# Post-norm work of the first tokens dealt out over the last FFN product, hidden pieces split earlier, and more matmuls between norm sums and their spread

## The chip, the core and the metric

The kernel runs on one core of a Trainium2 chip. A core has a matrix engine (TensorE, PE in the profile, its weight loads PEld), a vector engine (VectorE, DVE), a scalar engine (ScalarE, ACT), GpSimd (POOL) and SyncE (SP), each with an instruction queue of its own; they wait for one another through semaphores, and sixteen DMA engines move data. The metric is the device time of one execution in microseconds.

## What is computed

Two layers of a transformer over 512 tokens of width 1024, all in float32. Layer 0 attends with low-rank queries and keys (8 heads), layer 1 attends over chunks to keys and values projected once from the end of layer 0 (16 heads). Each layer ends in the same feed-forward network. Every sub-layer is normed before and after:

```python
for layer in range(DEPTH):
    h = rms_norm(x, attn_pre_g[layer])
    y = mla_mixer(h, ...) if layer < N_A_LAYERS else chunked_mixer(h, k_band, v_band, ...)
    x = x + rms_norm(y, attn_post_g[layer])
    h = rms_norm(x, ffn_pre_g[layer])
    f = swiglu(h, ffn_w_gate[layer], ffn_w_up[layer], ffn_w_down[layer])
    x = x + rms_norm(f, ffn_post_g[layer])
    if layer == N_A_LAYERS - 1:
        k_band, v_band = shared_kv(x, kv_src_g, w_kv_shared)
```

with `swiglu(h, g, u, d) = (silu(h @ g) * (h @ u)) @ d`, a hidden width of 2816, and `rms_norm(x, g) = x * rsqrt(mean(x*x) + 1e-6) * g`.

## The kernel before

**Products.** A float32 product is made of three matmuls (`mm3`, L351 to L354): both operands are split into a rounded half and the rest, high by high, low by high and high by low are added in PSUM. For that each weight is cast by ScalarE to `whi` (L144), and VectorE takes the rest, `wlo = w - whi` (L145). Where a gain is folded in, the same is done by L148 and L149. Activations are split likewise, as `xh`/`xl`, `th`/`tl` or `ph`/`pl`.

**The order.** The code is written as one program; a scheduler then sets the order of the instructions on each engine from the program's order and its own estimates, and each engine runs its queue strictly in that order. So an instruction that waits holds all that stands behind it on its engine. Generators (`some(gen, n)` runs n steps, `run(gen)` the rest; `Filler.step` one step) lay the matmuls of one product around other work.

**Norm sums.** A norm over the features needs a sum over partitions. VectorE adds squares into `acc` (L422), TensorE sums `acc` over partitions with transposes or ones (`tot`, L431), `rstd` (L436) makes `r` with GpSimd's power (L448), and `spread` (L461) transposes `r` back over all partitions (`bc`, L465). Between `tot` and `bc` stand a few matmuls of the running product: `add_half(h, banks, rest, n1, n2)` (L571) runs n1 steps ahead of the sum and n2 steps between sum and spread; in `ffn` (L1064) it is `some(rest, 4)`, and at the start of layer 1's values (L1435) `spread_sb(rtk)` comes as soon as `rtk` is there.

**The down product.** `down` (L1149) multiplies the hidden values by the down weights with seven products instead of eight of half the size, in the order A11, A22, A12, E1, E2, E3, E6 (j = 0 to 6). Each has six weight tiles in five groups, the last group with two, and is 66 matmuls of 128x512 into two PSUM banks (al, de, ga, be, al, al, be). Ahead of each tile `hid.ahead(n)` (L1104) splits the hidden pieces up to step n into `ph` and `pl`; before, n is two steps ahead. Behind each group the post-norm object is called with `during(j, i)`, and behind each product with `product(j, banks)`.

**The post-norm.** `After` (L1204) puts the seven products together: `copy` (L1218) takes a bank into `y`, `plus` (L1223) adds another and squares (`sq`, L1228). The tokens stand in four tiles of 128, the outputs in two halves o. Behind E3 the first two token tiles are whole: `plus(1, 0)`, `rstd(0)` and `plus(1, 1)` follow at once. `power` (L1257) makes `r` from the two sums (ssv, L1260 and L1261; power on GpSimd, L1263) and calls `scale`, in layer 0 on ScalarE (L1270). Then `turn(h)` (L1279) transposes the scaled y (`yt`, L1288) and adds it to x (L1291); `turn(0)` is called in E6 behind the fourth tile (i == 3), `turn(1)` inside the value product of layer 1 (L1425). The residual `x` comes back from memory by `fetch(a["mid"])` (L608), called in E1 at i == 3.

`AfterLast` (L1295), for layer 1, has no next product. It transposes the residual x into rows (`xt`, L1316, copied by L1318) during E2 at i = 1 to 4, two tiles a group, multiplies y by the gain (`yg`, L1322), and `scale` (L1335) multiplies by r, adds xt and stores a tile of 256 KB (L1336).

## Time and profile before

| | |
|---|---|
| three runs | 1150.61, 1150.11 and 1149.77 us, median 1150.11 |
| the profiled execution | 1152.78 us, its span 1151.0 us |
| mean granted TensorE clock | 0.992 |
| seven down products, layer 0 and 1 | the last of them is E6, 513.88 to 536.55 and 1119.77 to 1142.33 |
| data moved | 149.80 MB, 130 GB/s in the mean |

Times in the trace count from the start of the span. A row of the timeline has its start, its length, engine, line, operation, what it writes and reads, the shape and the number of like instructions merged in it; in brackets stands the idle time of the engine before it and what ended that. A row of the waits has who waited for whom, the sum, the number and the longest. A row of windows has the length, then for PE, PEld, DVE, ACT and POOL the busy time with the number of instructions, then the granted TensorE clock, the DMA share and GB/s. Matmuls are pipelined: one 128x512 is shown as 0.39 us long, and the next starts 0.23 us later.

### The profile page before, as it was taken

To read this page: it belongs to the slowest core of one execution; us is meant where nothing else is said; L and a number is where in the kernel's file an instruction comes from. 1 tells how busy PE (TensorE), PEld (TensorE's weight loads), DVE (VectorE), ACT (ScalarE), POOL (GpSimd) and SP (SyncE) were. 2 spreads that over 40 slices of the span, in tenths; PEclk is the share of its full clock that TensorE was granted. 3 is DMA by queue.
4 is the path that set the end of the run, shared out by engine and by line. 5 is a ranking of instruction groups with operands and counts; after the bars stand their busy time and mean duration, and the time that the engine had idled before them with its cause. 6 is when DMAs were issued, how large, how long until landed. Compare 5 with 4: busy or idle time off the path is not lost.

```text
span 1151.0 us, 18964 instructions
## 1 busy us (share of the span) xinstructions
PE 1120.8 (97%) x6973; PEld 993.7 (86%) x6973; DVE 936.2 (81%) x1674; ACT 684.1 (59%) x1335; POOL 63.2 (5%) x90
## 2 busy tenths in 40 slices
PE   9999999999999999999999999999999999999995
PEld 6888889899999998777788887789899999998774
DVE  7787638999898889878768877748999898889866
ACT  6476646755555566668436766655655555556662
POOL 1200000000000003300000000000000000004200
PEclk9999999999999999998999999999999999999998
DMA  7433134322323359922446656444323323369701
GB/s 230 119 108 100 38 120 173 128 74 93 129 92 123 97 172 252 235 67 95 137 135 163 171 151 166 128 165 138 101 93 102 102 92 129 102 219 230 164 1 74
DMA packets 62270, 149.80 MB, mean 130 GB/s; under 512 B 8352, under 2 KB 9888, under 8 KB 62176
## 3 DMA queue, kind: packets, MB, share of 16 engines
q1 hardware_dynamic: 55696, 137.00, 37.9%
q0 software_dynamic: 6336, 11.54, 6.1%
q8 instruction: 55, 0.90, 0.3%
q14 instruction: 39, 0.32, 0.1%
q10 hardware_dynamic: 144, 0.04, 0.0%
HBM read 119.52 MB, written 8.59 MB: 111 GB/s over the span
## 4 chain that ended last, share of the span: by engine, by line
PE 80%; DVE 8%; issue 5%; ACT 4%; DMA 2%; POOL 1%; SPq 0%; DVEq 0%; POOLq 0%; ACTq 0%
PE al L1366 18%; PE b L352 10%; PE b L353 10%; PE b L354 9%; PE be L1366 9%; PE al L1169 5%; PE ga L1366 5%; PE be L1169 3%; PE de L1169 2%; PE pt L504 2%; DVE wlo L145 2%; PE ga L1169 1%; ACT whi L144 1%; ACT p L492 1%; DVE pl L145 1%
## 5 line engine op out<-in xcount | busy, mean ns | idle before, releaser
L144 ACT CAST whi<-raw 128x1024 fp32r<-128x1024 f32 (+3 forms) x224 | 225.3, 1006 | 234.0 <-PE al L1366 82.9
L145 DVE TENSOR_TENSOR wlo<-raw,whi 128x1024 fp32r<-128x1024 f32 (+3 forms) x224 | 260.7, 1164 | 74.6 <-ACT whi L144 71.8
L1366 PE MATMUL al<-th,whi 128*128 128x256 f32 x432 | 124.1, 287 | 0.0
L1366 PE MATMUL al<-tl,whi 128*128 128x256 f32 x432 | 122.2, 283 | 0.0
L1366 PE MATMUL al<-th,wlo 128*128 128x256 f32 x432 | 122.1, 283 | 0.0
L352 PE MATMUL b<-xh,whi 128*128 128x512 f32 (+1 forms) x304 | 116.3, 385 | 0.4 <-ACT xh L148 0.3
L353 PE MATMUL b<-xl,whi 128*128 128x512 f32 (+1 forms) x304 | 113.0, 372 | 0.0
L354 PE MATMUL b<-xh,wlo 128*128 128x512 f32 (+1 forms) x304 | 112.9, 371 | 0.0
L174 DVE TENSOR_TENSOR raw<-raw,raw 128x1024 f32<-128x1024 f32 x72 | 86.5, 1217 | 0.2
L1366 PEld LDWEIGHTS al<-th,whi 128*128 128x128 f32 x432 | 82.7, 191 | 1.8
L1366 PEld LDWEIGHTS al<-th,wlo 128*128 128x128 f32 x432 | 82.8, 192 | 0.0
L1366 PEld LDWEIGHTS al<-tl,whi 128*128 128x128 f32 x432 | 82.7, 191 | 0.0
L492 ACT ACTIVATE p<-p,mn 128x128 f32<-128x128 f32 (+1 forms) x96 | 54.0, 562 | 31.6 <-DVE mn L490 31.2
L144 ACT CAST whi<-wd 128x512 fp32r<-128x512 f32 x86 | 50.0, 619 | 37.9 <-PE al L1169 13.7
L145 DVE TENSOR_TENSOR ptl<-pt,pth 128x128 fp32r<-128x128 f32 (+1 forms) x96 | 46.2, 485 | 28.7 <-ACT pth L144 23.1
L145 DVE TENSOR_TENSOR wlo<-wd,whi 128x512 fp32r<-128x512 f32 x86 | 56.2, 684 | 14.9 <-ACT whi L144 14.7
L354 PEld LDWEIGHTS b<-xh,wlo 128*128 128x128 f32 x304 | 57.5, 189 | 8.9
L352 PEld LDWEIGHTS b<-xh,whi 128*128 128x128 f32 x304 | 57.7, 190 | 8.6 <-ACT xh L148 1.7
L353 PEld LDWEIGHTS b<-xl,whi 128*128 128x128 f32 x304 | 57.7, 190 | 7.5 <-DVE xl L149 0.7
L144 ACT CAST pth<-pt 128x128 fp32r<-128x128 f32 (+1 forms) x96 | 40.3, 424 | 28.4 <-PE pt L504 27.7
L1169 PE MATMUL al<-whi,ph 128*128 128x512 f32 x132 | 52.0, 394 | 2.9 <-ACT y L1218 1.6
L1169 PE MATMUL al<-whi,pl 128*128 128x512 f32 x132 | 51.4, 392 | 0.2
(304 smaller groups left out, 3277.9 us busy)
## 6 DMA issues: line engine op xcount, KB each, us to landing
raw<-in_w_pair SPq DMA_DIRECT2D x72, 512.0 KB, 3.5
wd<-in_w_down SPq DMA_DIRECT2D x54, 256.0 KB, 6.0
raw<-in_w_o SPq DMA_DIRECT2D x16, 512.0 KB, 3.6
raw<-in_w_gu SPq DMA_DIRECT2D x16, 512.0 KB, 3.8
raw<-in_w_down SPq DMA_DIRECT2D x16, 512.0 KB, 4.4
raw<-in_w_qkb SPq DMA_DIRECT2D x16, 512.0 KB, 3.5
wd<-in_w_down POOLq DMA_DIRECT2D x22, 256.0 KB, 5.2
wd<-raw POOLq DMA_DIRECT2D x22, 256.0 KB, 5.3
```

Source lines behind the costliest of these rows:

```text
L144: return (nc.scalar.copy(dst_hi, src), V.tensor_tensor(dst_lo, src, dst_hi.bitcast(F32), op=OP.subtract))
L145: V.tensor_tensor(dst_lo, src, dst_hi.bitcast(F32), op=OP.subtract))
L174: V.tensor_tensor(t, x, y, op=OP.add)
L352: nc.tensor.matmul(o, l[0], r[0], start=start, stop=False)
L353: nc.tensor.matmul(o, l[0], r[1], start=False, stop=False)
L354: nc.tensor.matmul(o, l[1], r[0], start=False, stop=stop)
L492: nc.scalar.activation(p[:, :n], p[:, :n], AF.Exp, bias=mn[:, :1], scale=-1.0, accum_out=self.sums[:, qt:qt + 1])
L504: nc.tensor.transpose(t[:, kt * P:(kt + 1) * P], p[:, kt * P:(kt + 1) * P], ident)
L1169: nc.tensor.matmul(to[e], l[c], r[d], start=j < 4 and k == 0 and n == 0, stop=k == NF // 2 - 1 and n == 2, skip_group_check=True)
L1366: nc.tensor.matmul(o, l[c], r[d], start=first_ and n == 0, stop=k == K2 - 1 and n == 2, skip_group_check=True)
```

## The change

Five things are edited.

1. `add_half` in the output projection takes 8 and 5 steps in place of 5 and 7: three steps more ahead of the sum, two fewer between the sum and its spread.
2. In `ffn`, 7 steps in place of 4 stand between the sum of the pre-norm and its spread. The spread of `rtk` in layer 1 moves behind seven steps of the filler.
3. `hid.ahead` splits pieces three steps ahead in E2 and E3 and four steps ahead in E6, in place of two.
4. `After` puts `plus(1, 1)` and the scaling of the first two token tiles on a list, `later`; each group of E6 takes one of them off the list. `fetch` is called at i == 1 of E1.
5. `AfterLast` makes each pair of `xt` a group earlier, deals the work out as `After` does, multiplies the o = 1 half of the first two token tiles by its gain in `scale`, and scales and stores the very last tile in two halves.

```diff
-                    post.add_half(0, before, rest, 5, 7)
+                    post.add_half(0, before, rest, 8, 5)
...
-        some(rest, 4)
+        some(rest, 7)
         rb = spread_sb(r)
...
-                    hid.ahead(at + 2 - len(got))
+                    hid.ahead(at + (2, 2, 2, 2, 3, 3, 4)[j] - len(got))
...
             elif j == Down.E3:
                 self.plus(1, 0, banks)
                 self.rstd(0)
-                self.plus(1, 1, banks)
+                self.later = [lambda: self.plus(1, 1, banks)] + self.later
...
             for e in range(n):
-                self.scale(i + e, r[:, e:e + 1])
+                do = lambda e=e: self.scale(i + e, r[:, e:e + 1])
+                self.later.append(do) if i < 2 else do()
...
         def during(self, j, i):
-            if j == Down.E1 and i == 3:
+            if j == Down.E1 and i == 1:
                 self.x = fetch(a["mid"])
                 self.split = Split(self.x, None)
+            if j == Down.E6 and self.later:
+                self.later.pop(0)()
             if j == Down.E6 and i == 3:
                 self.turn(0)
...
-            super().during(j, -1 if j == Down.E6 else i)
+            super().during(j, min(i, 2))
...
-            if j == Down.E2 and i:
-                for n in {1: (0, 1), 2: (2, 3), 3: (4, 5), 4: (6, 7)}[i]:
+            if j == Down.E2 and i < 4:
+                for n in (2 * i, 2 * i + 1):
...
         def whole(self, o, i):
+            if o and i < 2:
+                return
+            self.gained(o, i)
+            if i >= 2 and not o:
+                self.power(i, 1)
+
+        def gained(self, o, i):
             t = U(name="yg")
             V.tensor_tensor(t, self.y[o][i], self.g[o], op=OP.mult)
             self.y[o][i] = t
 
-            if i >= 2 and not o:
-                self.power(i, 1)
...
         def scale(self, i, r):
-            for o in (1, 0) if i >= 2 else (0, 1):
+            if i < 2:
+                self.gained(1, i)
+            for o in (1, 0):
                 t = self.y[o][i]
-                V.scalar_tensor_tensor(t, t, r, self.xt[i][o], op0=OP.mult, op1=OP.add)
-                nc.sync.dma_start(out[:, i, o * S:o * S + S], t)
+                for c in HALF if i == 3 and not o else (ALL,):
+                    V.scalar_tensor_tensor(t[:, c], t[:, c], r, self.xt[i][o][:, c], op0=OP.mult, op1=OP.add)
+                    nc.sync.dma_start(out[:, i, o * S:o * S + S][:, c], t[:, c])
...
-    rb = spread_sb(rtk)
...
     fill = Filler(fill_b())
+    for _ in range(7):
+        fill.step()
+    rb = spread_sb(rtk)
```

How this moves instructions, at three places.

ScalarE in E6 of layer 0, before. `y_...<-y_...,r` are the scalings of the first two token tiles, `sq` the squares of y, `ph` the pieces of the coming tiles:

```order
L1228 ACTIVATE sq_5957,ss_0_5086<-y_5398 128x512
L1228 ACTIVATE sq_5968,ss_0_5086<-y_5701 128x512
L1228 ACTIVATE sq_5971,ss_0_5086<-y_5703 128x512
L1270 ACTIVATE y_5234<-y_5234,r_5961 128x512
L1270 ACTIVATE y_5396<-y_5396,r_5961 128x512
L1270 ACTIVATE y_5236<-y_5236,r_5961 128x512
L1270 ACTIVATE y_5398<-y_5398,r_5961 128x512
L144 CAST ph_5973<-hd_3081 128x256
L144 CAST ph_5973<-hd_3330 128x256
L144 CAST whi_6015<-wd_5262 128x512
```

The same place of the changed kernel:

```order
L144 CAST ph_5981<-hd_4816 128x256
L1228 ACTIVATE sq_6012,ss_0_5086<-y_5701 128x512
L144 CAST whi_6021<-wd_5262 128x512
L144 CAST whi_6021<-wd_5264 128x512
L1271 ACTIVATE y_5234<-y_5234,r_5967 128x512
L1228 ACTIVATE sq_6015,ss_0_5086<-y_5703 128x512
L144 CAST ph_6017<-hd_5077 128x256
L1271 ACTIVATE y_5396<-y_5396,r_5967 128x512
L144 CAST whi_6043<-wd_5290 128x512
L144 CAST whi_6043<-wd_5292 128x512
L1271 ACTIVATE y_5236<-y_5236,r_5967 128x512
L1271 ACTIVATE y_5398<-y_5398,r_5967 128x512
```

The four scalings now stand apart and behind six more casts of pieces. On TensorE the first transposes of the scaled y stand behind 48 matmuls of E6, before behind 12.

TensorE in the first products of layer 0's FFN; `tot` stands ahead of these rows, `bc` is the spread of the pre-norm's r. It is one piece of the difference:

```order
 L353 MATMUL b_2632<-xl_2232,whi_2375 128x512
 L354 MATMUL b_2632<-xh_2231,wlo_2376 128x512
-L465 MATMUL bc_2674<-ident,r_2658 128x128 x4
 L352 MATMUL b_2633<-xh_2231,whi_2375 128x512
 L353 MATMUL b_2633<-xl_2232,whi_2375 128x512
```

and nine matmuls further on:

```order
 L353 MATMUL b_2633<-xl_2238,whi_2636 128x512
 L354 MATMUL b_2633<-xh_2237,wlo_2637 128x512
+L465 MATMUL bc_2689<-ident,r_2658 128x128 x4
 L352 MATMUL b_2632<-xh_2243,whi_2636 128x512
 L353 MATMUL b_2632<-xl_2244,whi_2636 128x512
```

The spread moved behind nine more matmuls of the same product.

VectorE at the end of the program, before; `be` are the two banks of the last product, `yg` the output tiles:

```order
L1223 TENSOR_TENSOR y_12624<-y_12624,be_11828 128x512
L1322 TENSOR_TENSOR yg_12911<-y_12624,g_11858 128x512
L1261 SCALAR_TENSOR_TENSOR ssv_11823<-ss_1_11821,ssv_11823 128x1
L1335 SCALAR_TENSOR_TENSOR yg_12779<-yg_12779,r_12915,xt_12580 128x512
L1335 SCALAR_TENSOR_TENSOR yg_12911<-yg_12911,r_12915,xt_12573 128x512
L1223 TENSOR_TENSOR y_12626<-y_12626,be_11829 128x512
L1322 TENSOR_TENSOR yg_12924<-y_12626,g_11858 128x512
```

and in the changed kernel, with the dealt-out work of the sixth weight tile ahead of it:

```order
L1332 TENSOR_TENSOR yg_12868<-y_12139,g_11860 128x512
L1345 SCALAR_TENSOR_TENSOR yg_12297<-yg_12297,r_12768,xt_12523 128x512
L1345 SCALAR_TENSOR_TENSOR yg_12868<-yg_12868,r_12768,xt_12530 128x512
L145 TENSOR_TENSOR wlo_12875<-wd_12063,whi_12874 128x512
L1223 TENSOR_TENSOR y_12628<-y_12628,be_11828 128x512
L1223 TENSOR_TENSOR y_12630<-y_12630,be_11829 128x512
L1332 TENSOR_TENSOR yg_12911<-y_12628,g_11858 128x512
L1261 SCALAR_TENSOR_TENSOR ssv_11823<-ss_1_11821,ssv_11823 128x1
L1332 TENSOR_TENSOR yg_12924<-y_12630,g_11858 128x512
L1345 SCALAR_TENSOR_TENSOR yg_12815<-yg_12815,r_12915,xt_12564 128x512
L1345 SCALAR_TENSOR_TENSOR yg_12911<-yg_12911,r_12915,xt_12557 128x512
```

Both additions of the last banks now stand ahead of the scaling, and scalings of the first tokens stand between the last two `wlo`.

## The prediction

> **What bounds the kernel now.** I read first the page's busy line and its chain, then the list of waits, then windows of equal work beside each other. The page:

> ```profile
> span 1151.0 us, 18964 instructions
> PE 1120.8 (97%) x6973; PEld 993.7 (86%) x6973; DVE 936.2 (81%) x1674; ACT 684.1 (59%) x1335; POOL 63.2 (5%) x90
> PE 80%; DVE 8%; issue 5%; ACT 4%; DMA 2%; POOL 1%; SPq 0%; DVEq 0%; POOLq 0%; ACTq 0%
> ```

> TensorE is the bound: 97% busy, 80% of the chain. The change takes no matmul away, so it can only win idle time of TensorE, time in which its clock is low, or the tail behind the last matmul. The waits of TensorE, sums first, then the number of waits and the longest:

> ```profile
> PE yt L1288 <- ACT y L1270: 3.0, 3, 1.9
> PE bc L465 <- POOL r L448: 2.7, 2, 1.4
> PE be L1169 <- ACT ph L144: 2.1, 1, 2.1
> PE be L1169 <- DVE pl L145: 2.0, 1, 2.0
> PE al L1169 <- ACT y L1218: 1.6, 1, 1.6
> PE tot L431 <- DVE acc L422: 1.6, 1, 1.6
> PE al L1169 <- ACT ph L144: 1.3, 2, 1.0
> ...
> PE bc L465 <- DVE rtk L1434: 1.1, 1, 1.1
> ```

> These eight rows are 15.4 us, and each stands at a place that the diff touches. Beside them there is the clock. The rows below are windows: length, busy time of each engine with its instructions, and PEclk, the granted clock, as the first bare number behind POOL:

> ```profile
> 513.88:536.55 22.67, 20.04 (x83) 16.14 (x82) 17.73 (x41) 18.18 (x42) 1.37 (x4) 0.85 0.08 24
> 1104.69:1119.77 15.08, 15.08 (x67) 12.50 (x67) 10.61 (x18) 9.12 (x19) 0.00 (x0) 1.00 0.00 0
> 1119.77:1142.33 22.56, 18.45 (x67) 13.77 (x65) 16.23 (x34) 9.87 (x26) 1.16 (x2) 0.85 0.13 48
> 1100.00:1110.00 10.00, 8.36 (x41) 6.83 (x40) 7.29 (x12) 7.65 (x15) 0.00 (x0) 1.00 0.00 0
> ```

> The second is E3 of layer 1, 66 matmuls without a stall: 15.1 us, 0.227 each. The first and the third are the last product E6 of both layers, again 66 matmuls (in layer 0 with 16 transposes): 22.7 and 22.6 us. Each has idle time (22.67 - 20.04 = 2.6 and 22.56 - 18.45 = 4.1) and a clock of 0.85, which is 15% of 22.6, or 3.4 us, lost in each. These two stages are the heart of the change.

> **The change part by part.**

> *E6 of layer 0.* Why TensorE waits there shows on ScalarE:

> ```profile
> 516.16 0.61 ACT L1228 ACTIVATE sq<-y 128x512 f32<-128x512 f32 x1
> ...
> 517.88 2.56 ACT L1270 ACTIVATE y<-y,r 128x512 f32<-128x512 f32 x4 [0.39 <-POOL r L1263]
> 520.34 0.69 ACT L144 CAST ph<-hd 128x256 fp32r<-128x256 f32 x2
> 518.65 0.47 PE L1288 MATMUL yt<-ident,y 128*128 128x128 f32 x2 [1.89 <-ACT y L1270]
> ```

> The transposes yt stand behind 12 matmuls of E6, their scaled y comes at 518.5. In the new order 48 matmuls stand ahead of them: 48 x 0.227 = 10.9 us after 513.88, or 524.8. By then ScalarE, which in the new order casts pieces from 516.2 on, has seven ph (0.3 from one to the next), two squares (0.7 with their read), four whi (0.52) and the four y (0.64) behind it: 8.2 us, so 524.4. So the two waits (2.6) and, if it hangs on them, the low clock (3.4) go: about 6.0, E6 ends near 530.7. What is late next is the weight of the V product behind it. VectorE takes its x, xl and wlo first:

> ```profile
> 534.07 0.48 DVE L1291 SCALAR_TENSOR_TENSOR x<-yt,gains,x 128x256 f32<-128x256 f32 x1
> 534.46 0.41 DVE L145 TENSOR_TENSOR xl<-x,xh 128x256 fp32r<-128x256 f32 x1
> 535.52 0.74 DVE L149 SCALAR_TENSOR_TENSOR wlo<-raw,gains,whi 128x512 fp32r<-128x512 f32 x1
> ```

> From the first transposes (525) VectorE has 8 x (0.39 from one to the next), 5 xl (0.35) and one wlo (0.75) to do, 5.6 us, and of the last x two more waits for yt: wlo is there at 532.3, TensorE wants it at 531.2. I charge 1.2 for that, 0.8 for the second wlo (two later rows), and take back 0.3 for the wait of the next transposes (the third of the yt row). Net **4.3**, bounds 2.5 (low clock goes, all new waits doubled) and 6.3 (no new wait).

> *E6 of layer 1.* Here the pieces ph and pl of the second weight tile are late:

> ```profile
> 1123.76 2.74 DVE L1335 SCALAR_TENSOR_TENSOR yg<-yg,r,xt 128x512 f32<-128x512 f32 x4 [0.61 <-POOL r L1263]
> 1124.30 2.54 ACT L144 CAST ph<-hd 128x256 fp32r<-128x256 f32 x8
> 1127.02 1.43 DVE L145 TENSOR_TENSOR pl<-hd,ph 128x256 fp32r<-128x256 f32 x4
> ```

> Four scalings of the first tokens (2.74) and a gain stand ahead of pl on VectorE, three squares and two casts ahead of ph on ScalarE. In the new order the pieces of two tiles are made ahead of E6, six ph casts follow the second square, and the scalings stand behind 48 matmuls, one gain and two scalings a group. 4.1 idle and 3.4 of clock go, 7.5 in all. The dealt-out work has a price: summing VectorE's rows in the new order (pl 0.34, wlo and gain 0.60, scaling 0.65 from one to the next) from 1122.4 on, the wlo of the fifth tile is ready at 1131.0, wanted at 1130.9, that of the sixth at 1134.2, wanted at 1133.9. I charge 0.5 and take **7.0**, bounds 4 (VectorE 3 us later than summed) and 7.5.

> *Sums and their spread.* In both FFNs the transposes bc stand nine matmuls later (12 to 21 behind tot), 9 x 0.227 = 2.0:

> ```profile
> 219.62 0.39 PE L354 MATMUL b<-xh,wlo 128*128 128x512 f32 x1
> 221.38 0.65 PE L465 MATMUL bc<-ident,r 128*128 128x128 f32 x4 [1.37 <-POOL r L448]
> ```

> The gap is 1.37, so it goes in both layers: **2.7**. The price: gt, the first reader, comes 0.5 later on the clock while TensorE reaches the fourth product 1.5 sooner; hd of the first product was there some 2.4 before it, so up to 0.5 per layer may come back. For rtk ten more matmuls (2.3) cover 1.1: **1.1**; its readers, the V rows, come 1.2 later, with two more accumulators free to go on. In the output projection tot stands 2 matmuls later in layer 0 and 6 in layer 1, bc one later and three sooner. What ended the wait of 1.6 on acc in layer 1 was a cast ahead of it on ScalarE:

> ```profile
> 778.85 1.05 ACT L144 CAST whi<-raw 128x1024 fp32r<-128x1024 f32 x1 [2.20 <-DMA raw<-in_w_gu]
> ```

> The cast waits for a load that nothing here moves. Six more matmuls of 0.12 (128x256) can cover 0.7 of it: **0.7**, bounds -0.4 (the spread three sooner) and 1.6.

> *Pieces made earlier in E2 and E3, xt a group earlier.* The al<-ph waits (1.3, the larger 0.98 of layer 0) go: ph is asked for a tile earlier. The 1.6 at the start of E3 is this queue on ScalarE:

> ```profile
> 1101.52 1.66 ACT L144 CAST whi<-wd 128x512 fp32r<-128x512 f32 x3 [1.66 <-PE al L1169]
> 1103.09 1.06 ACT L1318 COPY xt<-xt 128x512 f32<-128x512 f32 x2
> 1104.04 1.08 ACT L1218 COPY y<-al 128x512 f32<-128x512 f32 x2
> ```

> In the new order the last two xt copies stand a group earlier, and y follows one cast. **1.3 + 1.6**. The price is x. The xt stand 18 matmuls earlier (4.1 us: six at 1079.3 instead of 1083.4), and they need x<-mid:

> ```profile
> 1069.56 6.76 SPq L608 DMA_DIRECT2D x<-mid  x8
> DMA to landing us min/median/max: 3.8/6.7/7.8
> ```

> Issues run from 1069.56 to 1076.32, so the last lands at about 1082. The fetch is asked for two groups earlier, on the same place of SP's queue; buffers let it go 1 to 4 us sooner. If the landings move by 1 us, the sixth tile is 0.4 late; if they don't, 1.5; if they move by 2, nothing. I charge **-0.4**.

> *Tail.* The last matmul and what VectorE does behind it:

> ```profile
> 1142.10 0.39 PE L1169 MATMUL be<-whi,pl 128*128 128x512 f32 x1
> 1140.48 0.69 DVE L1223 TENSOR_TENSOR y<-y,be 128x512 f32<-128x512 f32 x1 [3.37 <-PE be L1169]
> 1144.17 0.68 DVE L1223 TENSOR_TENSOR y<-y,be 128x512 f32<-128x512 f32 x1
> 1146.47 1.41 DVE L1335 SCALAR_TENSOR_TENSOR yg<-yg,r,xt 128x512 f32<-128x512 f32 x2 [0.67 <-POOL r L1263]
> ```

> Before, the first y runs ahead of the last nine matmuls' end, the second waits behind the scaling of the first; the last row ends 5.8 after the last matmul began. After, both y stand ahead of that scaling, but TensorE ends both halves within the last four matmuls, so the first y comes about when the last matmul starts. Chained by the same rows (y, y, gain, gain, power 0.55, two scalings, the next power, scaling and two halves) the last row ends about 6.1 behind. Storing the last tile in halves gives some 0.1 back. **-0.2**, bounds -0.8 and +0.8.

> **The sum.** 4.3 + 7.0 + 2.7 + 1.1 + 0.7 + 1.3 + 1.6 - 0.4 - 0.2 = 18.1 us. The profiled execution took 1152.78 (span 1151.0), so 1134.7 by it; the runs' median of 1150.11 lies 2.67 under it, which gives **1132.0 us**.

> [...] In this trace the low clock stands only where two waits of about 2 us lie close together (1.9 and 0.75; 2.1 and 2.0); the single wait of 1.6 in 1100 to 1110 left it at 1.00. [...]

> **Rivals.**

> *The clock stays low at both last products*, since its cause is not these waits, or since new waits of VectorE's rows (17.7 and 16.2 us of work in stages that shrink to 16.7 and 15.1) come as close together. For it: VectorE then fills these stages. Against it: the E3 window, the same matmuls at 1.00. Then 18.1 - 6.8 = 11.3, or 1138.8; with 1.5 for VectorE as the bound 1140.3.

> *It stays low at one of them*: 18.1 - 3.4 = 14.7, or 1135.4. The likelier place is the V product of layer 0, with two new waits of 1.2 and 0.8.

> *More than I sum*: no new wait in either E6 (+2.0 and +0.5), acc wholly covered (+0.9), x in time (+0.4), tail +1: 22.9, or 1127.2.

> *Slower, by x.* TensorE runs in order, so E2 stands still if x<-mid is late for the earlier xt. It costs what the sixth tile lands behind 1079.3. To eat 18.1 it would land at 1097.4, or with 3.4 of low clock at 1094; before, the last of the eight was there at about 1082. At that point it costs all that the rest wins (1150); by the rows it costs 1.5 at most, so it needs a queue 15 us longer than the one seen, from two groups of extra loads that the new order doesn't have.

> *It doesn't do what it says*: the scheduler could put the rows back. The new order shows them moved; left are waits that only change their releaser, 1150.

> **How the numbers follow.** Forecast near 1132 (1128.5 to 1134.5): 0.55. Low clock at one place: 0.18. At both: 0.12. More than summed: 0.10. Nothing: 0.02. Slower: 0.03, by x or a like queue. The range holds the first, the one-place and the more-than case (0.83). Its upper end takes in the lower bounds of both last products at once (1.8 and 3.0 less, 1136.8) and with them acc, x and the tail at their worst (1.1, 1.1 and 0.6, 1139.6), which I cut to 1139, as all five together are unlikely; below it ends at the more-than case: 1127 to 1139. A difference under 0.2% (2.3 us) can hardly be told from none: faster 0.95, same 0.02, slower 0.03.

> **What would show it.** Right: no yt or be wait over 1 us in E6 of either layer, E6 of layer 1 about 15.6 us at clock 1.00, E6 of layer 0 about 17, waits on L149's wlo of about 1 us behind it, no bc wait in the FFNs, E3 starting without the wait on y. Wrong: PEclk at 0.85 again in one of these stages; a wait of xt on x over 1 us; a new wait on gt or hd of the first FFN products; waits on wlo of over 2 us in E6 of layer 1, by which the dealt-out scalings would have replaced the stall that they left.

## The result

Five runs of the changed kernel took 1138.44 to 1140.33 us, median 1138.64; five of the kernel before 1149.77 to 1151.27, median 1150.61. The ratio is 0.9901, with an interval of [0.9886, 0.9915]: 12.0 us faster, where 18.1 were forecast. The median of 1138.64 lies just within the forecast's range of 1127 to 1139 and above the 1128.5 to 1134.5 of its likeliest case. The profiled execution took 1138.44 us, 14.3 less than the one of before.

### The profile page after: what moved, and what is told of

It is laid out like the page before. It is cut to its first block, busy times and chain, and to the rows that moved or that the text cites. A ratio compares the mean times of both kernels' runs of the same rounds, so it can differ in the third digit from the quotient of the medians.

```text
span 1136.7 us, 18969 instructions
## 1 busy us (share of the span) xinstructions
PE 1114.3 (98%) x6973; PEld 989.2 (87%) x6973; DVE 934.5 (82%) x1675; ACT 682.0 (60%) x1335; POOL 65.0 (6%) x90
## 4 chain that ended last, share of the span: by engine, by line
PE 86%; DVE 7%; ACT 3%; DMA 2%; issue 1%; POOL 1%; SPq 0%; DVEq 0%; POOLq 0%; ACTq 0%
PE al L1376 18%; PE b L352 11%; PE b L353 10%; PE b L354 10%; PE be L1376 9%; PE al L1169 8%; PE ga L1376 5%; PE be L1169 3%; PE pt L504 2%; PE de L1169 2%; DVE wlo L145 2%; PE ga L1169 1%; ACT whi L144 1%; DMA x<-mid 1%; PE b L1500 1%
## 5 line engine op out<-in xcount | busy, mean ns | idle before, releaser
L144 ACT CAST whi<-raw 128x1024 fp32r<-128x1024 f32 (+3 forms) x224 | 225.3, 1006 | 217.7 <-PE al L1376 74.8
L145 DVE TENSOR_TENSOR wlo<-raw,whi 128x1024 fp32r<-128x1024 f32 (+3 forms) x224 | 260.5, 1164 | 68.4 <-ACT whi L144 65.8
L354 PE MATMUL b<-xh,wlo 128*128 128x512 f32 (+1 forms) x304 | 112.7, 371 | 0.0
L145 DVE TENSOR_TENSOR ptl<-pt,pth 128x128 fp32r<-128x128 f32 (+1 forms) x96 | 46.2, 485 | 28.3 <-ACT pth L144 22.7
L354 PEld LDWEIGHTS b<-xh,wlo 128*128 128x128 f32 x304 | 57.4, 189 | 8.8
L144 ACT CAST whi<-wd 128x512 fp32r<-128x512 f32 x86 | 49.8, 619 | 24.8 <-PE de L1169 8.6
L145 DVE TENSOR_TENSOR wlo<-wd,whi 128x512 fp32r<-128x512 f32 x86 | 56.2, 684 | 8.3 <-ACT whi L144 7.9
L144 ACT CAST pth<-pt 128x128 fp32r<-128x128 f32 (+1 forms) x96 | 40.2, 423 | 28.7 <-PE pt L504 28.0
L1169 PE MATMUL al<-whi,ph 128*128 128x512 f32 x132 | 51.7, 392 | 0.0
L1169 PE MATMUL al<-whi,pl 128*128 128x512 f32 x132 | 51.6, 391 | 0.0
```

The costliest lines, as they stand in the source:

```text
L144: return (nc.scalar.copy(dst_hi, src), V.tensor_tensor(dst_lo, src, dst_hi.bitcast(F32), op=OP.subtract))
L145: V.tensor_tensor(dst_lo, src, dst_hi.bitcast(F32), op=OP.subtract))
L354: nc.tensor.matmul(o, l[1], r[0], start=False, stop=stop)
L1169: nc.tensor.matmul(to[e], l[c], r[d], start=j < 4 and k == 0 and n == 0, stop=k == NF // 2 - 1 and n == 2, skip_group_check=True)
```

## The profile after

These rows of the changed kernel's page answer to those of before:

```profile
span 1136.7 us, 18969 instructions
PE 1114.3 (98%) x6973; PEld 989.2 (87%) x6973; DVE 934.5 (82%) x1675; ACT 682.0 (60%) x1335; POOL 65.0 (6%) x90
PE 86%; DVE 7%; ACT 3%; DMA 2%; issue 1%; POOL 1%; SPq 0%; DVEq 0%; POOLq 0%; ACTq 0%
```

TensorE has the same 6973 matmuls and is 6.5 us less busy, since a matmul at clock 0.50 counts as busy for longer: in E6 of layer 0 before, from 521.64 on, a 128x512 is shown as 0.63 us long and the next starts 0.43 later, against 0.39 and 0.23 at 1.00. Its waits in the changed kernel (sum, times, longest):

```profile
PE be L1169 <- ACT ph L144: 1.7, 1, 1.7
PE bc L465 <- POOL r L448: 1.5, 2, 0.8
PE b L352 <- ACT xh L148: 1.3, 1, 1.3
...
PE b L353 <- DVE wlo L149: 1.1, 2, 0.6
PE xt L1319 <- DMA x<-mid: 0.9, 1, 0.9
...
PE tot L431 <- DVE acc L422: 0.4, 1, 0.4
PE yt L1291 <- ACT y L1271: 0.3, 1, 0.3
```

All eight rows of before are gone or changed: the first row here is a new wait, in E1 of layer 0, and the second is not the FFN's spread but the output projection's (0.83 in layer 0, 0.63 in layer 1). The third stands in the first product of the program, whose order is the same; its longest wait was between 0.3 and 1.8 in all traces. Both last products, as windows (length, busy times, clock behind POOL):

```profile
513.65:530.45 16.80, 16.80 (x83) 13.93 (x82) 14.66 (x33) 16.44 (x38) 1.23 (x4) 1.00 0.12 33
1111.77:1127.38 15.61, 15.51 (x67) 12.05 (x65) 14.71 (x30) 8.45 (x22) 0.83 (x1) 1.00 0.19 69
```

22.67 became 16.80, 22.56 became 15.61, both without a gap of note and at clock 1.00. Measured between the same matmuls of both traces, the 14.3 us come from these places:

| place | forecast | measured |
|---|---|---|
| E6 of layer 0, with the V product behind it | -4.3 | -5.9 + 1.8 = -4.1 |
| E6 of layer 1 | -7.0 | -7.1 |
| spread in both FFNs | -2.7 | -1.8 - 1.2 = -3.0 |
| spread of rtk | -1.1 | -1.2 |
| output projection, layer 0 | 0 | +0.7 |
| output projection, layer 1 | -0.7 | -0.4 |
| E1 to E3 of layer 0 | -1.0 | +1.2 - 0.5 = +0.7 |
| E1 to E3 of layer 1 | -1.5 | +1.3 - 2.3 = -0.9 |
| behind the last matmul's start | +0.2 | +0.8 |
| the rest | 0 | +0.2 |
| sum | -18.1 | -14.3 |

## The experiments

All start from the changed kernel, but for three traces of the kernel before near the end. Differences under 1 us are read from stages of the traces, since the executions of one kernel lie 1.0 to 4.7 us apart.

**Where the new wait in E1 comes from.** On ScalarE it looks like this in the changed kernel, with the TensorE row that waits below:

```profile
477.42 1.04 ACT L144 CAST whi<-raw 128x1024 fp32r<-128x1024 f32 x1 [2.05 <-PE be L1169]
478.37 1.45 ACT L144 CAST ph<-hs 128x512 fp32r<-128x512 f32 x3
479.03 0.50 PE L1169 MATMUL be<-whi,ph 128*128 128x512 f32 x1 [1.66 <-ACT ph L144]
```

A weight cast waits for a matmul, and three ph of the same product stand behind it. First the fetch of layer 0 was put back to the fourth group:

```diff
-            if j == Down.E1 and i == 1:
+            if j == Down.E1 and i == (1 if self.layer else 3):
```

> The changed kernel, but layer 0 asks for its residual x at the fourth group of E1 again, as before the change. The trace of the changed kernel has a new wait of 1.7 us in E1 of layer 0 (be on ScalarE's ph), and two ph casts there stand behind a cast that itself waits for a matmul. Theory: the eight x tiles, taken two groups earlier, hold the buffers that ph needs. Then the wait goes, E1 of layer 0 is 1.2 to 1.8 us shorter, and nothing else moves by over 0.3: time 1.2 to 1.8 us under the changed kernel. Rival: the pieces asked for three steps ahead in E2 push these casts back; then the wait of about 1.7 stays and the time with it.

Measured: the median was 1139.31, so the time that was expected did not come. The wait of 1.66 is gone, E1 is 1.2 shorter, as the theory has it; but the wait of 0.98 at the start of E2, which the change had removed, is back, and E2 with E3 is 0.5 longer. The rival falls, as the wait went although the pieces were still asked for three steps ahead. What the theory had missed is that both waits move with the fetch. Then the fetch went on to the second group of E2:

```diff
-            if j == Down.E1 and i == 1:
+            if (j, i) == ((Down.E1, 1) if self.layer else (Down.E2, 1)):
```

> The changed kernel, but layer 0 asks for x at the second group of E2, so that neither E1 nor the start of E2 has eight x tiles in the buffers (x is first read in E6). Theory: the waits on ph around the end of E1 (1.66 in the changed kernel, 0.98 with the fetch at the fourth group of E1) are one want of buffers that moves with the fetch; now neither is there, E1 and E2 with E3 of layer 0 together 1.4 to 1.9 us shorter than in the changed kernel. Rival: the want of buffers only moves on, into E2 or E3, as a wait of 1 us or more there; time within 0.5.

E1 of layer 0 in the changed kernel, and in this one:

```profile
466.17:483.68 17.51, 15.71 (x68) 12.09 (x66) 13.35 (x21) 10.59 (x20) 6.14 (x7) 1.00 1.08 247
```

```profile
466.22:481.39 15.17, 15.17 (x68) 12.25 (x66) 13.29 (x21) 10.49 (x20) 6.17 (x7) 1.00 0.81 137
```

The same 68 rows take 2.3 us less, more than the theory has, without an idle moment, and E2 and E3 don't give it back: median 1137.49, ratio 0.9881 [0.9865, 0.9897]. So x, asked for before E2, is what makes ph late in layer 0. ScalarE's queue in this run shows how:

```profile
473.04 0.40 ACT L144 CAST ph<-hs 128x256 fp32r<-128x256 f32 x1
...
475.36 0.61 ACT L144 CAST ph<-hs 128x512 fp32r<-128x512 f32 x1
477.50 1.05 ACT L144 CAST whi<-raw 128x1024 fp32r<-128x1024 f32 x1 [1.53 <-PE be L1169]
```

These two ph and one at 471.48 stand ahead of the weight cast that waits for a matmul. In the changed kernel these three stand behind it, though ScalarE was idle for 1.77 and 2.05 ahead of it. So it isn't ScalarE's time that was short, but the order that was worse. The reason offered is that x takes eight tiles out of the 40 that x, ph, pl, y and sq share, long before E6 reads them, so that the scheduler had no free tile for ph. It is argued from the order alone; no run had a larger pool.

**The steps around the output projection's sum.**

```diff
-                    post.add_half(0, before, rest, 8, 5)
+                    post.add_half(0, before, rest, 5, 7)
```

> The changed kernel with 5 and 7 steps around the sum of the output projection, as before the change. Theory: in the changed kernel the spread, which has two steps fewer to hide in, waits 0.83 us in layer 0 and 0.63 in layer 1, while the wait of layer 1's sum fell from 1.60 to 0.38. Undone: layer 0 wins 0.6 to 0.9, layer 1 loses 0.4 to 0.8, in sum -0.5 to +0.2 us against the changed kernel. Rival: the sum of layer 1 waits for a load alone, which came earlier in this execution by chance; then layer 1 loses nothing and the time is 1.2 to 1.5 under the changed kernel.

Layer 0: the spread wait of 0.83 is gone, 0.7 won, as the theory has it. Layer 1: the sum waits 1.32 again, the spread no longer, and between the same matmuls the projection is 0.1 longer; another 1.0 is lost ahead of it, in the attention, half of it in one wait on a load. The loss of 0.4 to 0.8 that the theory has for layer 1 isn't there. Over all traces layer 1's projection lies between 0.4 under and 0.3 over the changed kernel's with 5 and 7 steps, and between 0.2 under and 0.4 over with 8 and 5, so neither pair is shown to be better there. The median (1138.53) can't tell it. This execution also showed a low clock in E1, below. Then each layer got its own steps:

```diff
-                    post.add_half(0, before, rest, 8, 5)
+                    post.add_half(0, before, rest, *post.steps)
...
+        post.steps = ((5, 7), (8, 7))[i]
```

> The changed kernel with 5 and 7 steps around the sum of the output projection in layer 0, and 8 and 7 in layer 1. Theory: the steps cover two waits of their own, sum and spread: layer 0 has no wait at the sum with 5 and none at the spread with 7; in layer 1 8 leave 0.3 to 0.6 at the sum and 7 nothing at the spread. The two spread waits (0.83 and 0.63) go: time 1.0 to 1.6 us under the changed kernel. Rival: the sums in layer 1 wait on a load that sets the pace, so that a wait spared at the spread comes back at the next sum; then 0.4 to 0.9.

Layer 0 wins 0.7. In layer 1 no sum waits, but a wait of 0.6 stands at the next half's spread, and the first products of layer 1's FFN, whose matmuls the scheduler put in another order, are 1.1 us longer. It doesn't look like chance: in the two later runs with 8 and 7 steps they are 0.9 and 1.0 longer, and in the nine other traces that have the changed kernel's edits of the FFN they are equal to its own within 0.02. So these steps lose in layer 1, which neither theory nor rival has. The median, 1139.65, shows no gain.

**The dealing and the earlier splitting, each alone.** First without the dealing:

```diff
-                self.later = [lambda: self.plus(1, 1, banks)] + self.later
+                self.plus(1, 1, banks)
...
-                self.later.append(do) if i < 2 else do()
+                do()
```

> The changed kernel without the dealing out: the second addition behind E3 and the scaling of the first two token tiles are written right behind E3 as before, the pieces are still split three and four steps ahead. Theory: the dealing is what frees VectorE and ScalarE in E6. Undone, in layer 1 four scalings and the gains stand ahead of the second half of the second tile's wlo: a wait of 4 to 6.5 us there, and the granted clock falls to 0.8 to 0.85 in that stage (another 3.4); in layer 0 a wait of 1 to 2 on pieces; time 7 to 12 us over the changed kernel. Rival: the earlier splitting alone removes the waits of E6; then E6 is within 1 us of the changed kernel in both layers, at clock 1.00.

```profile
PE be L1169 <- DVE wlo L145: 5.9, 1, 5.9
```

```profile
514.37:532.02 17.65, 17.34 (x84) 13.94 (x82) 14.89 (x35) 16.86 (x39) 1.49 (x4) 1.00 0.10 31
1111.69:1135.68 23.99, 18.08 (x67) 14.07 (x65) 16.06 (x32) 9.35 (x24) 1.34 (x2) 0.86 0.12 45
```

The first fence is of the waits, the second of windows over both E6. In layer 1 the second tile's wlo is 5.9 late and the clock falls: 8.4 us more than in the changed kernel. In layer 0 E6 is 0.9 longer and the V product 1.1 shorter: there the dealing is worth nothing, since pieces split ahead already put 24 matmuls in front of the transposes. Median 1145.93, ratio 0.9955 [0.9940, 0.9970]. The theory holds for layer 1, and its wait on pieces in layer 0 did not come. Then the dealing alone:

```diff
-                    hid.ahead(at + (2, 2, 2, 2, 3, 3, 4)[j] - len(got))
+                    hid.ahead(at + 2 - len(got))
```

> The changed kernel with pieces split two steps ahead everywhere, as before the change, and the dealing kept. Theory: the pieces of the second tile of E6 stand behind the second square on ScalarE and are there about 1 us late in layer 1; one wait of 0.5 to 1.3 us, too short and alone to lower the clock, no wait in layer 0's E6: time 0.5 to 1.6 us over the changed kernel, clock of both E6 stages 1.00. Rival: the splitting ahead carries half of the win; then waits of 2 us or more come back in layer 1 with a low clock, 4 to 7 us over the changed kernel.

E6 of layer 1 is 0.7 longer, E6 of layer 0 the same, clock 1.00 in both; the wait is on wlo and not on ph. Median 1139.39, as expected. In layer 1 the dealing carries the win, the earlier splitting 0.7; in layer 0 either is enough.

**xt.** A group later again, with x still fetched early:

```diff
-            if j == Down.E2 and i < 4:
-                for n in (2 * i, 2 * i + 1):
+            if j == Down.E2 and i:
+                for n in (2 * i - 2, 2 * i - 1):
```

> The changed kernel with the xt transposes a group later again (fetch of x still at the second group of E1). Theory: the earlier xt pay 0.9 us of waiting for x<-mid and win the wait of 1.6 us on y at the start of E3. Undone: the wait on x (0.5 to 0.9) goes and a wait of 0.6 to 1.6 on y returns, because the last xt copies stand ahead of y on ScalarE again; time -0.3 to +0.9 us against the changed kernel. Rival: the wait on y went by the pieces split earlier, not by xt; then no wait on y and time 0.5 to 0.9 under the changed kernel.

A wait of 1.39 on y is back at the start of E3, and E2 with E3 is 1.4 longer; the rival falls, and xt a group earlier is what removed the wait on y. The median was 1140.60, ratio 0.9908 [0.9891, 0.9924], which can't be told from the changed kernel's 0.9901. The wait on x did not go: xt waits 1.36. But it costs nothing. E1 of layer 1 takes 17.8 us in all twelve traces that ask for x there at the second group of E1, whether xt waits for x or not. The changed kernel first, then the run with the later fetch in layer 0, at the same place of layer 1:

```profile
1073.78 0.33 PE L1319 MATMUL xt<-ident,x 128*128 128x128 f32 x1 [0.86 <-DMA x<-mid]
1071.82 0.50 PE L1169 MATMUL be<-whi,ph 128*128 128x512 f32 x1 [1.04 <-ACT ph L144]
```

Where x is in time, TensorE waits for ph instead, which stands behind a waiting weight cast as in layer 0. Then xt in E3, x asked for at the second group of E2 in both layers:

```diff
-            if j == Down.E1 and i == 1:
+            if j == Down.E2 and i == 1:
...
-            if j == Down.E2 and i < 4:
+            if j == Down.E3 and i < 4:
```

> The changed kernel with x asked for at the second group of E2 in both layers and the xt transposes of layer 1 in the first four groups of E3 (they are first read in E6). Theory: the wait of 0.9 to 1.4 us around the end of E1 in layer 1 (xt on x, or ph) is the same want of buffers and landing time as in layer 0, and goes; E1 of layer 0 wins 2.3 as shown; E3 may lose 0.3 to 0.8 to the xt copies ahead of pieces on ScalarE. Time 2.3 to 3.3 us under the changed kernel. Rival: x and xt, held in E3, take the buffers that E6's pieces need; then a wait of 1 us or more in E6 of layer 1 and a time within 1.5 us of the changed kernel.

E1 of layer 1 has no wait, on ph or x: 2.5 shorter, part of it xt work that moved on; E2 with E3 1.1 longer, E6 0.4 longer: net -1.0, beside the 2.4 in layer 0. The rival's wait in E6 doesn't come. Median 1135.53, ratio 0.9863 [0.9845, 0.9882], 3.1 under the changed kernel's, as the theory has it.

**The tail.** In the changed kernel VectorE, then GpSimd, behind the last matmul (start 1127.03):

```profile
1127.00 1.28 DVE L1223 TENSOR_TENSOR y<-y,be 128x512 f32<-128x512 f32 x2 [0.69 <-PE be L1169]
1129.99 1.41 DVE L1345 SCALAR_TENSOR_TENSOR yg<-yg,r,xt 128x512 f32<-128x512 f32 x2 [0.44 <-POOL r L1263]
1132.14 1.54 DVE L1345 SCALAR_TENSOR_TENSOR yg<-yg,r,xt 128x512 f32<-128x512 f32 x3 [0.67 <-POOL r L1263]
1129.03 0.93 POOL L1263 TENSOR_TENSOR r<-ssv,mhalf 128x1 f32<-128x1 f32 x1 [13.56 <-DVE ssv L1261]
```

The last row of VectorE ends 6.65 behind that start; 6.1 was forecast, 5.78 was before. The first power took 0.93 instead of 0.55. One power for both tiles:

```diff
-            if i >= 2 and not o:
-                self.power(i, 1)
+            if i == 3 and not o:
+                self.power(2, 2)
```

> The changed kernel with one power for the last two token tiles of layer 1 instead of two. Theory: the tail from the start of the last matmul to the end of the last scaling is 6.65 us because the second sum stands behind the first tile's scalings on VectorE and waits for GpSimd once more; with one power it is y, y, gain, gain, one power, four scalings: 5.4 to 5.8 us, and the time 0.7 to 1.3 us under the changed kernel. Rival: the four stores then come at once and queue, and the last lands as late as before; time within 0.3.

```profile
1132.87 2.87 DVE L1345 SCALAR_TENSOR_TENSOR yg<-yg,r,xt 128x512 f32<-128x512 f32 x5 [0.81 <-POOL r L1263]
1132.14 0.70 POOL L1263 TENSOR_TENSOR r<-ssv,mhalf 128x2 f32<-128x2 f32 x1 [14.17 <-DVE ssv L1261]
```

From the last matmul (1129.52) to the end of the last scaling it is 6.22, not 5.4 to 5.8: both gains stand ahead of the one sum. 0.4 is won behind the last matmul in every run that has it; under what was expected, over the rival. The median doesn't show it: 1140.45, ratio 0.9908 [0.9893, 0.9923], which can't be told from the changed kernel's 0.9901; in the traced execution E1 of layer 0 lost 1.6 to a low clock, of which more below.

**The spread in the FFNs and of rtk, put back.**

```diff
-        some(rest, 7)
+        some(rest, 4)
...
     V.tensor_copy(rtk, rt)
+    rb = spread_sb(rtk)
...
-    for _ in range(7):
-        fill.step()
-    rb = spread_sb(rtk)
```

> The changed kernel with the spread of both FFN pre-norms and of rtk put back to where they stood (4 steps; at once). Theory: the waits return in full (1.4 twice and 1.1, and nothing was paid for the cover), so the time is 3.4 to 4.2 us over the changed kernel. Rival: the later spread cost as much at its readers as it covered in part; then 1.5 to 3.

```profile
PE bc L465 <- POOL r L448: 4.3, 4, 1.4
...
PE bc L465 <- DVE rtk L1444: 0.9, 1, 0.9
```

The span is 3.9 longer, median 1143.18 (ratio 0.9925 [0.9910, 0.9940]). The waits grow by 2.8 and 0.9, so nothing was paid for the cover; the later readers had time.

**What wins, joined.** First the fetch of layer 0 at E2, steps by layer, one power:

> The changed kernel with three corrections joined: layer 0 asks for x at the second group of E2, 5 and 7 steps around the sum of layer 0's output projection and 8 and 7 in layer 1, one power for the last two token tiles. Theory: each is its own stall on TensorE or in the tail, so they add: 2.3 (E1 of layer 0) + 0.65 (layer 0's spread) + 0.4 (tail) and 0 to 0.4 in layer 1, that is 3.3 to 3.8 us off the span of the changed kernel, about 1134.8 to 1135.3 us if no load is late by chance. Rival: what is won ahead is lost at the next wait on a load; then under 2 us.

Median 1136.15, ratio 0.9865 [0.9849, 0.9882]; the span was 2.4 under the changed kernel's. E1 and the projection of layer 0 and the tail give 2.4 + 0.7 + 0.4 = 3.5, the theory's numbers; against it stands above all the 0.9 that layer 1's steps cost in its FFN. With x at E2 and xt in E3 in layer 1 as well:

> All that won, joined: x asked for at the second group of E2 in both layers, xt in E3, 5 and 7 steps (layer 0) and 8 and 7 (layer 1) around the sum of the output projection, one power for the last two token tiles. Theory: the stalls are separate and add: E1 of layer 0 2.4, E1 to E6 of layer 1 1.0, layer 0's spread 0.6, tail 0.4, layer 1's sum 0 to 0.4: 4.4 to 4.8 us under the changed kernel, a median of 1133.8 to 1134.6. Rival: the tail and E6 share VectorE, so the tail's 0.4 goes; then 3.6 to 4.0.

```profile
PE b L352 <- ACT xh L148: 1.1, 1, 1.1
PE b L353 <- DVE wlo L149: 1.0, 2, 0.6
...
PE bc L465 <- POOL r L448: 0.6, 1, 0.6
```

No wait on ph or x is left. Median 1135.06, ratio 0.9868 [0.9850, 0.9887]; the span of 1133.1 is 3.5 under the changed kernel's, short of the 4.4 to 4.8 of the theory, with 1.0 lost to layer 1's steps again. The tail's 0.4 is there, against the rival. No run has the rest with 8 and 5 steps in layer 1. The times of this kernel and the two ahead of it can't be told apart.

**How much clock the kernel before loses.** The two traces differ by 14.3, the medians by 12.0. Four more executions were traced, three of the kernel before and one of the changed kernel, with no edit:

> The kernel before, unchanged, a second look. Theory: the clock falls for 3.4 us or a multiple of it when TensorE was busy for under half of one free-running window of 3.41 us, so the same stalls cost 0, 1.7 or 3.4 us of clock by where they lie; the two E6 stages together then show another loss than 6.8 in at least one of three looks, and the span moves with it by as much. Rival: the stalls of E6 lower the clock for 6.8 us in both layers each time; spans within 1 us of 1151.0.

> As the look before it: a third look at the kernel before, with the same two theories.

> As the look before it: a fourth look at the kernel before, with the same two theories.

> The changed kernel, a second look. Theory: its stall of 1.7 us in E1 of layer 0 lowers the clock for one window in some executions (1.7 us more, mean clock 0.996) and not in others (0.998), by the busy share of the window that it falls in; nothing in E6. Rival: the executions at 0.996 lose their clock in E6; then a low window stands there.

The spans of before were 1147.6, 1148.7 and 1151.2 (the first profile: 1151.0). In E6 of layer 1 the clock was halved for 6.8 us in all four. In layer 0 it wasn't in the first of the three, for 3.4 in the second, for 6.8 in the third and in the first profile; E6 there took 20.2, 21.5, 22.6 and 22.7, with the same idle time of 2.6 to 2.7. E6 of layer 0 in the first of the three:

```profile
513.83:534.04 20.21, 17.51 (x84) 13.91 (x82) 17.47 (x41) 18.16 (x42) 1.36 (x4) 1.00 0.08 27
```

So 6.8 us of half clock cost 2.5 there, and 3.4 us cost 1.3, each time less than half of the stretch, presumably because TensorE would have waited for part of it at full clock too. In the first profile of before the clock falls at 518.92, at 1126.49 and, behind the last matmul, at 1146.97: 607.57 and 20.48 us apart, 178 and 6 steps of 3.413 us. Low stretches inside the products lasted 3.41 or 6.83 us. Windows of this length, laid from such an edge of the same trace, show what went ahead of a fall. The first profile of before, the 3.41 us ahead of a fall in layer 0 and in layer 1:

```profile
515.50:518.92 3.42, 1.53 (x8) 0.92 (x6) 2.43 (x6) 3.03 (x9) 1.37 (x4) 1.00 0.01 2
...
1123.08:1126.49 3.41, 0.73 (x2) 0.30 (x2) 2.80 (x6) 3.41 (x12) 0.65 (x1) 1.00 0.34 124
```

The first of the three again, where layer 0 kept its clock, and the second, where it fell for one window:

```profile
514.81:518.22 3.41, 1.91 (x9) 1.25 (x7) 3.08 (x7) 3.02 (x9) 1.36 (x4) 1.00 0.01 2
518.22:521.64 3.42, 2.23 (x12) 1.51 (x12) 1.23 (x4) 3.42 (x8) 0.00 (x0) 1.00 0.00 0
```

```profile
516.21:519.63 3.42, 0.78 (x4) 0.20 (x2) 1.52 (x5) 3.03 (x8) 1.36 (x4) 1.00 0.01 2
519.63:523.04 3.41, 3.38 (x11) 3.00 (x12) 2.44 (x7) 3.41 (x10) 0.00 (x0) 0.50 0.02 5
```

And the changed kernel around its one stall of 1.66 in E1, in the first profile and in the second:

```profile
476.11:479.52 3.41, 1.75 (x8) 1.17 (x7) 1.68 (x3) 2.10 (x4) 1.84 (x4) 1.00 1.11 199
479.52:482.93 3.41, 3.27 (x15) 2.37 (x14) 1.74 (x4) 0.88 (x2) 0.86 (x1) 1.00 1.04 211
```

```profile
478.03:481.44 3.41, 1.61 (x6) 0.89 (x6) 2.09 (x4) 2.40 (x4) 1.79 (x3) 1.00 0.82 142
481.44:484.86 3.42, 3.42 (x9) 2.64 (x9) 0.67 (x2) 0.40 (x1) 0.83 (x1) 0.50 0.94 219
```

Read the second number, TensorE's busy time. After a window of 1.53, 0.73, 0.78 or 1.61 of 3.41 (21 to 47%) the clock was 0.50 in the next, and so it was after 1.54 in the third of the three, in E6 of layer 0, and after 1.61 in the run with 5 and 7 steps, in E1; after 1.91, 2.23 and 1.75 (51 to 65%) it was 1.00. What a window between 1.61 and 1.75 does is not shown by these. The edge ahead of the stall in E6 of layer 0 stood at 515.50 in the first profile of before and at 514.81, 516.21 and 516.04 in the three others, and the same waits came with 6.8, 0, 3.4 and 6.8 us of half clock. The theory holds for where the clock falls, though the loss in time is 0, 1.3 or 2.5 and not 0, 1.7 or 3.4; the rival, a fixed loss in both layers, does not hold. For the changed kernel the second trace's span is 1138.9 at a mean clock of 0.996, the first's 1136.7 at 0.998, and E1 of layer 0 took 19.1 in place of 17.5; it took 19.1 too in the two other traces with a low window there.

## Why the forecast held and where it didn't

The forecast of 18.1 was 6.1 too large. 3.8 of it lie between its sum and the 14.3 of the two traces, mostly in the pieces of E1 to E3 (2.3), the output projection (1.0) and the tail (0.6). The other 2.3 lie between the two traces and the medians: the profiled execution of before, 1152.78, was slower than all five runs.

**Both last products: right in mechanism.** 4.1 against 4.3 and 7.1 against 7.0. The transposes wait 0.3, the pieces are in time, the clock stays at 1.00, and the late wlo of the V product showed as two gaps of 0.6 and 0.5 and a stage 1.8 longer. The dealing alone explains layer 1 (8.4 us when undone). In layer 0 my reason was too wide: either half of the change would have done. And its number is partly luck: of the 5.9 that E6 lost, 2.6 were idle time, as forecast, but 2.5 and not 3.4 were the clock. The last 0.7 is in no term of the sum: TensorE is busy for 17.5 us in that stage with the waits, even at full clock, and for 16.8 without them.

**That the clock hangs on the waits: right, its size wrong.** The step that failed is the sentence that 15% of 22.6 us, or 3.4, is lost in each of the two stages. Against the trace in which layer 0 kept its clock, it was 2.5 there in the profiled execution itself, and 2.5, 1.3 and 0 in the three others, but the sum took it over to the median in full. In layer 1 the clock was low for 6.8 us in all four traces, so what that costs in time can't be read apart from the waits. The changed kernel, for its part, loses 1.6 in some executions to the stall in E1. Four spans of before from 1147.6 to 1151.2 and two of after (1136.7 and 1138.9) lie 8.7 to 14.5 apart; the medians' 12.0 lies among them. The forecast's rivals on the clock asked in which stage it stays low, and should have asked in how many executions. Of these rivals the first, with the clock low at both last products and a sum of 11.3, is out: the clock is 1.00 at both in the changed kernel, so the loss did go with the waits.

**The pieces in E1 to E3: wrong, the largest miss.** The step was that the al<-ph waits of 1.3 go, since "ph is asked for a tile earlier". They went, and ph came late at another place: E1 of layer 0 is 2.3 us longer than with the fetch at E2. I priced the earlier fetch by what waits for x, and not by what it does to the order of ph on ScalarE. +0.7 in place of -1.0 is 1.7 of the 3.8 by which the traces miss the sum. In layer 1 the wait on y went as forecast, by the earlier xt. The term of 0.4 for x was put on the wrong tile: x was late by 0.9 in this execution and in time in others, but ph is late by 1.0 at that place in any case; -0.9 in place of -1.5.

**The spreads: right.** 3.0 and 1.2 against 2.7 and 1.1, with no price at the readers: the 0.5 a layer that might have come back did not. Undone, they cost 2.8 and 0.9 of waits and 3.9 of span.

**The output projection: a term left out.** Two steps fewer ahead of the spread were priced for layer 1 only. In layer 0 the sum had no wait to cover, and the spread then waited 0.83: +0.7. The fewer steps alone don't explain that: without its wait the spread would stand 2.17 us behind the sum, and before it stood 2.00 behind it and did not wait. What came later is r, from GpSimd's power, before and after:

```profile
182.90 0.70 POOL L448 TENSOR_TENSOR r<-v,mhalf 128x2 f32<-128x2 f32 x1 [125.78 <-DVE v L444]
183.11 1.75 POOL L448 TENSOR_TENSOR r<-v,mhalf 128x2 f32<-128x2 f32 x1 [125.91 <-ACT whi L144]
```

It took 1.75 in all ten traces with 8 steps ahead of this sum and 0.70 in all eight with 5; in layer 1, with a spread wait of 0.63, 1.5 to 1.7 in the thirteen with 8 and 0.70 in the five with 5. In the long ones VectorE splits a weight beside it for 1.0 to 1.2 us, in the short ones it works for 0.3 at most. That this is what lengthens the power was not tested. In layer 1 the 0.7 was 0.4 in these two traces, and over all of them nothing that can be told from chance.

**The tail: right in direction, small in size.** 6.65 against 6.1: GpSimd's power took 0.93 where I put 0.55, here too with VectorE at work beside it (the second gain), and halves cost 0.13 on VectorE.

## What to carry to other kernels

A fetch moved ahead has a price beside its landing: it can change the order of other work on an engine that it doesn't run on. Look at what shares its buffers at that place, ph here, even if that reason is only argued so far. Work dealt out over a product paid where an engine's queue was the bound of that product (VectorE in layer 1, 8.4 us), and nothing in layer 0, where pieces split ahead already put 24 matmuls in front of the transposes. A loss of clock read from one profile is one draw (0, 1.3 or 2.5 us in E6 of layer 0): trace more executions before it goes into a sum, and lay windows of 3.41 us over the stalls; here the clock fell after those with TensorE busy for 1.61 or less. A step count moved around a small GpSimd instruction also changes what VectorE does beside it (a split of 1.2 us beside the power in layer 0's projection, 0.3 of one before).
